# A two-layer hybrid block on one core: the state-space branch in groups of four time steps, every projection as three rounded products

## The chip, the cores and the metric

The kernel runs on one core of a Trainium2 chip. The core has a matrix engine (TensorE, PE in the profile, with its weight loads as PEld), a vector engine (DVE), a scalar engine (ACT), GpSimd (POOL) and a queue engine (SP) that issues most of the DMAs. Each engine works through its own queue in order and waits on semaphores for the others. The metric is the device time of one execution in microseconds (us); less is better.

## The reference

The input is 512 tokens of width 1024 with 16 learned tokens in front, all in 32-bit floating point. Two layers follow. Each layer normalizes, multiplies by `w_in` (1024 x 1376) and splits the result into three branches. Their results are normalized, joined, multiplied by `w_out` and added to the residual; then an MLP (1024 to 4096 and back, squared ReLU) follows. The branch that the change rewrites is the state-space one:

```
bu_re = einsum('blgc,gpc->blgp', uf, bb_re)      # 16 groups x 16 channels -> 64 states each
bu_im = einsum('blgc,gpc->blgp', uf, bb_im)
...
_, _, xr, xi = lax.associative_scan(_complex_affine_combine, (a_t_re, a_t_im, bu_re, bu_im), axis=1)
y = einsum('gcp,blgp->blgc', c_re, xr) - einsum('gcp,blgp->blgc', c_im, xi) + d_skip * uf
z = gelu(y);  out = z * sigmoid(z @ w_glu + b_glu)
```

So each complex state follows x[t] = lambda * x[t-1] + B u[t], one lambda for each of the 1024 states, and y[t] is the real part of C x[t], plus d u[t]. The other two branches are attention within a window of 128 and latent attention over all earlier tokens. Three of the gains in the inputs are some 3 to 8 times as large as usual, so that rounding shows in the output.

## The kernel before

Activations lie transposed: 128 features on the partitions, time along the free axis. The 528 rows of time (16 + 512) are two halves of 272 and 256, here called A and B (`hf` 0 and 1). Weights come from HBM in blocks of 128 output features. A block is two half-blocks, each a tile `raw` of 128 x 512 (256 KB) fetched by SP; there are 600 such loads.

`gemm` has two forms. In the **rounded** form a weight half-block is first split by `load_half`: ACT rounds it (`w` hi, line 123 by way of `act`), DVE subtracts to get the rest (`w` lo, line 132). The activation has been split likewise (`split`, `gains`). Three products per 128 features then run with rounded operands: hi*hi, hi*lo, lo*hi, so 12 matmuls per half-block (line 160). In the **exact** form, taken when the activation tile is plain F32, the 4 matmuls of a half-block run on unsplit 32-bit operands (line 152); no split is needed, and the profile shows each such matmul as two. Constants `FULL_IN`, `FULL_OUT` and `FULL_C0` say where the exact form stands: `w_in` of layer 0 for both halves (9 of 11 blocks for A, 11 for B), `w_out` for half A in both layers, and the first chunk of the MLP for half A in both layers. That makes 68 blocks or 136 half-blocks, 544 matmuls (1088 in the profile), 78 half-blocks of them before 295 us. After the first chunk `resplit` makes the split activation.

`s5_prep` builds, from 8 columns of parameters, a table `tab` of cos and sin for 272 time steps and the input matrices `b3`. `s5_half` then treats the 1024 states as 8 tiles of 128 and one time half at a time. For each tile: two matmuls make B u (line 472, from `u3`, a split copy of u made by ACT and line 466); DVE turns it by the table into real recurrences (lines 477 to 480), runs two scans along all time steps (line 485), turns back (488 to 491), and matmuls with C give y (line 497).

Order: `weave` emits a main stream of projection blocks and, between them, steps of two side streams, `s5_half` and `attn_half`, at rates `RS` and `RA`; the yields say what a step costs. The tile framework then orders instructions by priority and by free buffers; weight splits and norm chains carry a raised priority (`HW`, `HP`). The stages used below are: `w_in` A (0 to 54 us); `w_in` B woven with the branches of A (54 to 160); `w_out` A, first MLP chunk of A, woven with the branches of B (160 to 295); the rest of layer 0's MLP (295 to 590); then for layer 1 `w_in` A and a rest of layer 0 with the branches of A (590 to 750), `w_in` B, `w_out` A, MLP of A with the branches of B (750 to 970), and the MLP to the end.

Of the kernel before, what the change touches and what calls it, by code (L numbers as in the profile page):

```python
# [20 lines left out]
P = 128  # L21
# [24 lines left out]
TAB = 272  # L46
# [20 lines left out]
def hybrid(ctx, tc, xT, wblk, small, wglu, wuq, wukv, bD, cD, ident_d, bias_d, tbias_d, mask_d, rope_d, tau_d, outT):  # L67
# [26 lines left out]
    def f32(ap):  # L94
        return ap.bitcast(F32)
# [144 lines left out]
    def s5_prep(L):  # L240
# [17 lines left out]
        tau = tmp_p()[:, 0]  # L258
# [5 lines left out]
        for i in range(8):  # L264
            act(tab[:, 1, i, :], tau, scale=phi[:, i:i + 1])
        for i0 in range(0, 8, 2):
            x = tab[:, 1, i0:i0 + 2, :]
            km = tmp_q()
            V.tensor_scalar(km, x, MAGIC, None, op0=ALU.add)
            V.scalar_tensor_tensor(x, km, MAGIC, x, op0=ALU.subtract, op1=ALU.subtract)  # L270
            for i in range(i0, i0 + 2):
                V.scalar_tensor_tensor(tab[:, 1, i, :], tau, plo[:, i:i + 1], tab[:, 1, i, :], op0=ALU.mult, op1=ALU.subtract)
            V.tensor_scalar(km, x, MAGIC, None, op0=ALU.add)
            V.scalar_tensor_tensor(x, km, MAGIC, x, op0=ALU.subtract, op1=ALU.subtract)
# [4 lines left out]
        for i in range(0, 8, 4):  # L279
            x = tab[:, 0, i:i + 4, :]  # L280
            act(x, x, AF.Square)
            V.tensor_scalar(x, x, -2.0, 1.0, op0=ALU.mult, op1=ALU.add)
        ar, ai = sm(l, "are"), sm(l, "aim")
        nr, ni, den, cr, ci = t8("nr"), t8("nim"), t8("den"), t8("cr"), t8("ci")
        V.tensor_tensor(nr, r, tab[:, 0, :, 1], op=ALU.mult)
        V.tensor_scalar(nr, nr, 1.0, None, op0=ALU.subtract)
        V.tensor_tensor(ni, r, tab[:, 1, :, 1], op=ALU.mult)
# [5 lines left out]
        V.tensor_tensor(b, ni, ai, op=ALU.mult)  # L293
        V.tensor_tensor(cr, a, b, op=ALU.add)
        V.tensor_tensor(cr, cr, den, op=ALU.mult)
        V.tensor_tensor(a, ni, ar, op=ALU.mult)
# [3 lines left out]
        crb = cr.unsqueeze(2).to_broadcast([P, 8, 32])  # L300
        cib = ci.unsqueeze(2).to_broadcast([P, 8, 32])
        b3 = mk(mem, [96, 2, 8, P], F32R, "b3")
        braw = tmp_p().rearrange("p a t -> p (a t)")[:, :512].rearrange("p (c i j) -> p c i j", c=2, i=8)
        t12 = tmp_q().rearrange("p a t -> p (a t)")[:, :512].rearrange("p (c i j) -> p c i j", c=2, i=8)
        t1, t2 = t12[:, 0], t12[:, 1]
        nc.gpsimd.dma_start(out=braw, in_=bD[l])
        for c in range(2):
            hi = mk(wk, [P, 8, 32], F32R, "u3")
            V.tensor_tensor(t1, braw[:, c], crb, op=ALU.mult)
            V.tensor_tensor(t2, braw[:, 1 - c], cib, op=ALU.mult)  # L310
            V.tensor_tensor(t1, t1, t2, op=ALU.subtract if c == 0 else ALU.add)
            act(hi, t1)
            for q in range(2):
                iq = slice(4 * q, 4 * q + 4)
                bb = tmp_p().rearrange("p a t -> p (a t)")[:, :384].rearrange("p (i j c) -> p i j c", i=4, j=3)
                act(bb[:, :, 0, :], f32(hi[:, iq]))
                act(bb[:, :, 1, :], f32(hi[:, iq]))
                V.tensor_tensor(bb[:, :, 2, :], t1[:, iq], f32(hi[:, iq]), op=ALU.subtract)
                ps = mk(psm, [P, 512], F32, "pt")
                for j in range(4):  # L320
                    PE.transpose(ps[:96, j * P:(j + 1) * P], bb[:, j].rearrange("p a b -> p (a b)"), ident)
                act(b3[:, c, iq, :], ps[:96].rearrange("p (j m) -> p j m", j=4))
        ct = mk(mem, [P, 2, 8, 32], F32, "ct")
        nc.gpsimd.dma_start(out=ct, in_=cD[l])
        L["s5"] = dict(r=r, tab=tab, b3=b3, ct=ct)
# [40 lines left out]
    def w_in(L, hf, ar, M):  # L366
# [17 lines left out]
        for b in range(NB_IN):  # L384
# [3 lines left out]
            if b < 2:  # L388
                scaled(M["u"][:, b, :n], ps[:, :n])
# [650 lines left out]
```

## Time and profile before

| | us |
|---|---|
| median of 3 runs | 1323.53 (1322.12 to 1324.77) |
| profiled execution, first to last instruction | 1320.8 |
| PE busy | 1246.2 (94%) |
| DVE busy | 911.0 (69%) |
| ACT busy | 830.8 (63%) |
| mean DMA rate | 129 GB/s |

No time of the profiled execution other than its span is recorded; the median stands 2.7 us above it. A line of the grouped view ends in "busy, mean ns of one | idle before". The matmul lines count a 32-bit matmul twice. Matmuls overlap, so their mean length is longer than the distance from one to the next; the timeline gives the distance, as a run of so many in so many us.

### The profile page before, as it was taken

The page shows a single profiled execution, that of the slowest core. Times are in us where ns is not written, and L with a number is a line of the kernel's source. Part 1 is how long each engine was busy: PE and PEld are TensorE (multiplying, and loading weights), DVE is VectorE, ACT ScalarE, POOL GpSimd, SP SyncE. Part 2 cuts the span into 40 slices and gives each one's busy share as a digit, 9 for nine tenths or more (in the row PEclk, how much of TensorE's full clock was granted, in tenths as well). Part 3 has the DMA queues.
Part 4 walks back from the last instruction along what each step waited for, and adds up shares of the span by engine and source line. Part 5 has one row for each costly group of instructions (what it writes and reads, how often), then busy time and mean ns, then how long its engine had stood idle before and what let it go on. Part 6 is the DMA issues. An engine that isn't in the chain of part 4 may idle for free.

```text
span 1320.8 us, 24423 instructions
## 1 busy us (share of the span) xinstructions
PE 1246.2 (94%) x8760; PEld 1106.6 (84%) x8760; DVE 911.0 (69%) x2234; ACT 830.8 (63%) x1959; POOL 30.3 (2%) x64
## 2 busy tenths in 40 slices
PE   6999897999999999899999997999899999999985
PEld 5866664779999999898889987767789999999985
DVE  8699888757756656868998668796575333334776
ACT  5855758587765656856878656477676542534663
POOL 3001000000000000000000000000000000000000
PEclk9999999999999999899999998999899999999998
DMA  7422131345666666464344654312346433334653
GB/s 233 142 80 65 57 88 33 90 131 154 183 184 176 176 175 174 133 178 118 113 129 136 185 141 138 112 56 73 105 127 198 117 93 96 97 96 123 188 178 96
DMA packets 93240, 170.55 MB, mean 129 GB/s; under 512 B 10832, under 2 KB 14032, under 8 KB 93120
## 3 DMA queue, kind: packets, MB, share of 16 engines
q1 hardware_dynamic: 90288, 161.72, 43.0%
q0 software_dynamic: 2832, 7.28, 1.8%
q8 instruction: 69, 1.13, 0.4%
q14 instruction: 51, 0.42, 0.1%
HBM read 166.87 MB, written 2.10 MB: 128 GB/s over the span
## 4 chain that ended last, share of the span: by engine, by line
PE 73%; DVE 13%; ACT 10%; issue 2%; DMA 2%; DVEq 0%; ACTq 0%; POOLq 0%
PE d L160 45%; PE d L152 9%; PE bu L160 7%; PE o L703 2%; PE pt L679 2%; PE y L497 2%; ACT ch L123 2%; ACT slot L123 2%; DMA raw<-in_wblk 1%; PE s L623 1%; DVE big L730 1%; PE s L655 1%; DVE wQ L485 1%; DVE h L731 1%; ACT w L123 1%
## 5 line engine op out<-in xcount | busy, mean ns | idle before, releaser
L160 PE MATMUL d<-slot,w 128*128 128x256 f32 (+1 forms) x5568 | 704.5, 286 | 24.4 <-ACT ch L123 6.7
L160 PEld LDWEIGHTS d<-slot,w 128*128 128x128 f32 x5568 | 682.6, 190 | 39.6 <-ACT slot L123 8.4
L123 ACT ACTIVATE w<-raw 128x512 fp32r<-128x512 f32 x464 | 290.9, 628 | 255.4 <-PE d L160 182.5
L132 DVE TENSOR_TENSOR w<-raw,w 128x512 fp32r<-128x512 f32 x464 | 319.0, 690 | 183.5 <-ACT w L123 177.4
L152 PE MATMUL d<-slot,raw 128*128 128x256 f32 (+1 forms) x1088 | 272.0, 393 | 12.3 <-DMA raw<-in_wblk 10.5
L152 PEld LDWEIGHTS d<-slot,raw 128*128 128x128 f32 x1088 | 202.1, 192 | 55.7 <-ACT ch L123 10.5
L167 DVE TENSOR_TENSOR slot<-rl,slot 128x256 fp32r<-128x256 f32 (+1 forms) x112 | 47.1, 426 | 65.5 <-ACT slot L123 64.9
L160 PE MATMUL bu<-slot,w 128*128 128x256 f32 x768 | 92.2, 279 | 0.0
L160 PEld LDWEIGHTS bu<-slot,w 128*128 128x128 f32 x768 | 90.8, 188 | 0.0
L123 ACT ACTIVATE rl<-d 128x256 f32<-128x256 f32 (+1 forms) x112 | 42.1, 376 | 31.4 <-PE d L152 15.1
L197 DVE TENSOR_TENSOR ch<-ch 128x256 f32<-128x256 f32 (+1 forms) x112 | 47.4, 424 | 14.2 <-ACT ch L123 12.6
L123 ACT ACTIVATE slot<-rl 128x256 fp32r<-128x256 f32 (+3 forms) x128 | 52.7, 420 | 2.8
L123 ACT ACTIVATE slot<-h,small 128x256 fp32r<-128x256 f32 (+3 forms) x88 | 39.6, 503 | 14.3 <-DVE h L731 10.3
L123 ACT ACTIVATE ph<-pt 128x512 f32<-128x512 f32 (+2 forms) x66 | 36.4, 552 | 18.9 <-PE pt L679 13.8
L123 ACT ACTIVATE rl<-rl 128x256 f32<-128x256 f32 (+1 forms) x112 | 45.9, 418 | 2.1
L801 DVE TENSOR_TENSOR big<-d,big 128x256 f32<-128x256 f32 (+1 forms) x80 | 34.2, 428 | 15.0 <-PE d L160 11.8
L123 ACT ACTIVATE big<-d 128x256 f32<-128x256 f32 (+1 forms) x64 | 23.8, 373 | 19.7 <-PE d L152 13.3
L655 PE MATMUL s<-kv,slot 96*128 96x264 f32 (+3 forms) x80 | 27.0, 419 | 5.8 <-DVE mx L534 5.8
L123 ACT ACTIVATE ch<-big 128x256 f32<-128x256 f32 (+1 forms) x64 | 26.2, 412 | 9.4 <-DVE big L801 7.2
L623 PE MATMUL s<-kv,slot 128*128 128x512 f32 (+1 forms) x64 | 31.3, 570 | 0.8 <-DVE mx L534 0.5
L123 ACT ACTIVATE u<-slot 32x272 fp32r<-32x272 f32 (+1 forms) x64 | 26.9, 420 | 4.9 <-PE bu L472 2.3
L731 DVE SCALAR_TENSOR_TENSOR h<-big,small,h 128x256 f32<-128x256 f32 (+1 forms) x64 | 28.4, 481 | 0.0
(583 smaller groups left out, 1242.3 us busy)
## 6 DMA issues: line engine op xcount, KB each, us to landing
raw<-in_wblk SPq DMA_DIRECT2D x600, 256.0 KB, 2.7
ph<-in_wuq POOLq DMA_DIRECT2D x8, 256.0 KB, 3.1
h<-in_xT SPq DMA_DIRECT2D x4, 272.0 KB, 4.0
h<-in_xT SPq DMA_DIRECT2D x1, 1024.0 KB, 12.4
ph<-in_wukv POOLq DMA_DIRECT2D x4, 256.0 KB, 3.4
u<-in_wglu POOLq DMA_DIRECT2D x4, 256.0 KB, 3.1
out<-h SPq DMA_DIRECT2D x1, 1024.0 KB, 5.6
out<-h SPq DMA_DIRECT2D x4, 256.0 KB, 2.1
```

Of the source, the lines that this page charges most:

```text
L123: S.activation(out, in_, func, **kw)
L132: V.tensor_tensor(w[:, 1].rearrange("p k m -> p (k m)"), raw, f32(hi), op=ALU.subtract)
L152: PE.matmul(ps[:, :n], lhsT=raw[:, k * P:(k + 1) * P], rhs=a[:, 4 * q + k, :n], start=q + k == 0, stop=q + k == 4)
L160: PE.matmul(ps[:, :n], lhsT=w[:, wi, k, :], rhs=a[:, ai, 4 * q + k, :n], start=i == 0, stop=i == 23)
L167: V.tensor_tensor(lo, src, f32(hi), op=ALU.subtract)
L197: V.tensor_tensor(acc, acc, sq, op=ALU.add)
L497: PE.matmul(yps[j:j + 32, :n], lhsT=s5["ct"][:, c, i - 1 + e, :], rhs=xs[e][:, c, :n], start=c == 0, stop=c == 1, tile_position=(0, j))
L623: PE.matmul(sp[:, :2 * nk].rearrange("p (e k) -> p e k", e=2), lhsT=M["q"][:, c0:c0 + P], rhs=L["k2"][:, :, ks:ks + nk], start=True, stop= ...
L655: PE.matmul(sp, lhsT=M["qh"][0:96, 2 * g + e, o:o + P], rhs=L["kh"][:, 2 * g + e, c0:c1], start=True, stop=True)
L679: PE.transpose(pt[:, 256 * x + P * e:256 * x + P * e + P], vs[e][:, c0:c0 + P], ident)
L731: V.scalar_tensor_tensor(h[hf][:, k, o:o + n], src[:, k, :n], sm(l, gn, k), h[hf][:, k, o:o + n], op0=ALU.mult, op1=ALU.add)
L801: V.tensor_tensor(ac[:, b, :n], ps[:, :n], ac[:, b, :n], op=ALU.add)
```

## The change

Two things change together. First, the three `FULL_` constants become empty, so that every block of `gemm` takes the rounded form: 600 half-blocks are split by ACT and DVE, before it was 464. Second, `s5_prep` and `s5_half` work on groups of four time steps (`CL`): u is laid out by step within the group, a matmul with slices of the identity stacks the four steps on the partitions, the scan runs over 68 or 64 groups, four tiles side by side in one instruction (its multiplier is zero at each tile's start), and y within a group comes from a matrix `tt` for the inputs of the group and four matrices `vt` for the state before it. The table shrinks from 272 to 72 columns; `s5_prep` multiplies out lambda's powers on DVE (`cmul`). These matmuls are plain 32-bit ones. The rates `RS` change too.

```diff
-FULL_IN = ((0, 0), (0, 1))
-FULL_OUT = ((0, 0), (1, 0))
-FULL_C0 = ((0, 0), (1, 0))
-RS = ((5.4, 3.56), (1.8, 4.4))
+FULL_IN = ()
+FULL_OUT = ()
+FULL_C0 = ()
+RS = ((2.4, 1.5), (0.75, 2.2))
...
-TAB = 272
+CL = 4
+TAB = 72
...
+        def cmul(dst, src, fr, fi, iq):
+            ni = iq.stop - iq.start
+            pq = flat(tmp_q(), 128 * ni)
+            p4, q4 = (pq[:, 64 * ni * e:64 * ni * e + 64 * ni].rearrange("p (c i j) -> p c i j", c=2, i=ni) for e in range(2))
...
+            for c in range(2):
+                V.tensor_tensor(p4[:, c], src[c], frb, op=ALU.mult)
+                V.tensor_tensor(q4[:, c], src[c], fib, op=ALU.mult)
+            V.tensor_tensor(dst[0], p4[:, 0], q4[:, 1], op=ALU.subtract)
+            V.tensor_tensor(dst[1], p4[:, 1], q4[:, 0], op=ALU.add)
...
+        for i0 in range(0, 8, 4):
+            iq = slice(i0, i0 + 4)
+            ws = [flat(tmp_p(), 512).rearrange("p (i s j) -> p i s j", i=4, s=CL) for _ in range(2)]
+            at = lambda m: [w[:, :, CL - 1 - m, :] for w in ws]
+            cmul(at(0), [braw[:, c, iq] for c in range(2)], cr, ci, iq)
+            for m in range(1, CL):
+                cmul(at(m), at(m - 1), lr, li, slice(i0, i0 + 4))
             for c in range(2):
                 ps = mk(psm, [P, 512], F32, "pt")
                 for j in range(4):
...
+                    PE.transpose(ps[:, j * P:(j + 1) * P], ws[c][:, j].rearrange("p a b -> p (a b)"), ident)
+                act(wt[:, c, iq, :], ps.rearrange("p (j m) -> p j m", j=4))
...
+        for m in range(CL):
+            for i0 in range(0, 8, 4):
+                iq = slice(i0, i0 + 4)
+                cmul([vt[:, m, c, iq] for c in range(2)], [vt[:, (m - 1) % CL, c, iq] for c in range(2)], lr, li, iq)
...
+        for o in range(2):
+            ups = mk(psm, [P, 512], F32, "y")
+            for j in range(4):
+                for q in range(CL):
+                    PE.matmul(ups[32 * q:32 * q + 32, j * K:j * K + K], lhsT=ident[:, 32 * j:32 * j + 32],
+                              rhs=M["u"][:, o, q * K:q * K + K], start=True, stop=True, tile_position=(0, 32 * q))
+            act(u4[:, o, :n], ups[:, :n])
...
             for c in range(2):
-                iv = 0.0 if hf == 0 else it[:, c, i:i + 1]
-                V.tensor_tensor_scan(v_[:, c, :n], rb, w_[:, c, :n], iv, op0=ALU.mult, op1=ALU.add)
...
+                V.tensor_tensor_scan(v_[:, c, :n], rs[:, 4 * o * K:4 * o * K + n], w_[:, c, :n], 0.0, op0=ALU.mult, op1=ALU.add)
...
+            for q in range(CL):
+                for m in range(3):
+                    for j in range(4):
+                        i = 4 * o + j
+                        if m == 0:
+                            lt, rh = s5["tt"][:, i, q, :], u4[:, o, j * K:j * K + K]
+                        else:
+                            lt, rh = s5["vt"][:, q, m - 1, i, :], x_[:, m - 1, j * K:j * K + K]
+                        PE.matmul(yps[32 * j:32 * j + 32, q * K:q * K + K], lhsT=lt, rhs=rh, start=m == 0, stop=m == 2,
+                                  tile_position=(0, 32 * j))
```

The scheduler's order changes with it. On PE, at the end of `w_in` A of layer 0 (`d_347` is its last block, `d_613` and `d_709` the first of B, `pt` the transposes of `s5_prep`), there stood before:

```order
L160 MATMUL d_347<-slot_293,w_350 128x272 x12
L160 MATMUL d_347<-slot_293,w_367 128x272 x12
L202 MATMUL d_601<-ch_584,ones 128x256
L202 MATMUL o_665<-am_663,ones 128x272
L152 MATMUL d_613<-slot_575,raw_614 128x256 x4
L152 MATMUL d_613<-slot_575,raw_620 128x256 x2
L321 MATMUL pt_523<-ident,wP_519 96x128 x4
L152 MATMUL d_613<-slot_575,raw_620 128x256 x2
L321 MATMUL pt_533<-ident,wP_529 96x128 x4
L152 MATMUL d_709<-slot_575,raw_710 128x256 x2
```

In the changed kernel, at the same place (`pt` the transposes of `s5_prep`, `y_707` the product that gives `tt`; the fence begins behind the first three sets of these), there stand:

```order
L341 MATMUL pt_794<-ident,wP_759 128x128 x4
L494 MATMUL y_966<-slot_159,ident 32x68
L203 MATMUL d_914<-ch_897,ones 128x256
L161 MATMUL d_926<-slot_880,w_929 128x256 x12
L161 MATMUL d_926<-slot_880,w_946 128x256 x12
L494 MATMUL y_966<-slot_159,ident 32x68 x15
L161 MATMUL d_1066<-slot_880,w_1069 128x256 x5
L494 MATMUL y_984<-slot_159,ident 32x68 x16
```

All 20 rows of the transposes and of `tt` now stand between the last block of A and the norm sum `d_914` that the first block of B needs; before, blocks of B stood between the transposes.

On DVE, in the same place of the program, before (`slot` u and the branch inputs, `wP`, `wQ` the state-space temporaries; no weight split stands here):

```order
L371 TENSOR_TENSOR slot_610<-d_613,rc_600 128x256
L562 SCALAR_TENSOR_TENSOR slot_151<-slot_151,small_92,am_663 128x272
L466 TENSOR_TENSOR u_95_628<-slot_151,u_95_628 32x272 x2
L477 TENSOR_TENSOR wP_639<-bu_636,tab_444 128x544
L478 TENSOR_TENSOR wQ_640<-bu_636,tab_444 128x544
L479 TENSOR_TENSOR wP_639<-wP_639,wQ_640 128x272
```

And in the changed kernel (`vt` the output matrices of `s5_prep`, `ch` the norm sum of half B, `w_929` the first weight split of B):

```order
L316 TENSOR_TENSOR wQ_822<-vt_697,lam_679 128x128
L198 TENSOR_TENSOR ch_897<-ch_897 128x256
L133 TENSOR_TENSOR w_929<-raw_927,w_929 128x512
L198 TENSOR_TENSOR ch_897<-ch_897 128x256
L317 TENSOR_TENSOR vt_697<-wQ_822 128x128
L198 TENSOR_TENSOR ch_897<-ch_897 128x256
L318 TENSOR_TENSOR vt_697<-wQ_822 128x128
L198 TENSOR_TENSOR ch_897<-ch_897 128x256
```

The norm sum and the first split of B now stand among the 96 small products of `s5_prep`, 58 of which lie ahead of the norm sum's first row.

## Rows read from the trace of the kernel before

**Rows 1.** The page: the span, then busy time, share and count of PE

```profile
span 1320.8 us, 24423 instructions
PE 1246.2 (94%) x8760; PEld 1106.6 (84%) x8760; DVE 911.0 (69%) x2234; ACT 830.8 (63%) x1959; POOL 30.3 (2%) x64
```

**Rows 2.** The page: the chain that ended last, shares by line

```profile
PE d L160 45%; PE d L152 9%; PE bu L160 7%; PE o L703 2%; PE pt L679 2%; PE y L497 2%; ACT ch L123 2%; ACT slot L123 2%; DMA raw<-in_wblk 1%; PE s L623 1%; DVE big L730 1%; PE s L655 1%; DVE wQ L485 1%; DVE h L731 1%; ACT w L123 1%
```

**Rows 3.** Busy time by stretch: PE, PEld, DVE, ACT, POOL, then PE's granted clock

```profile
0.00:54.00 54.00, 42.02 (x195) 35.27 (x196) 39.01 (x134) 35.19 (x68) 13.66 (x31) 1.00 0.69 212
54.00:160.00 106.00, 97.85 (x523) 67.05 (x524) 93.25 (x307) 68.92 (x207) 6.08 (x12) 0.98 0.22 65
160.00:295.00 135.00, 126.12 (x630) 89.53 (x628) 101.93 (x312) 97.64 (x246) 5.24 (x11) 0.96 0.30 86
295.00:590.00 295.00, 287.14 (x2228) 280.78 (x2228) 199.83 (x384) 195.99 (x415) 1.05 (x2) 0.99 0.61 170
590.00:750.00 160.00, 158.63 (x1217) 140.66 (x1216) 136.92 (x349) 118.30 (x303) 2.17 (x4) 1.00 0.46 134
750.00:970.00 220.00, 206.11 (x1249) 169.63 (x1248) 152.17 (x386) 136.90 (x336) 2.13 (x4) 0.96 0.38 109
970.00:1321.00 351.00, 328.36 (x2729) 323.64 (x2727) 187.88 (x365) 177.87 (x389) 0.00 (x0) 0.98 0.45 128
```

**Rows 4.** Groups by line: weight splits on ACT and DVE, u's copy on ACT

```profile
L123 ACT ACTIVATE w<-raw 128x512 fp32r<-128x512 f32 x464 | 290.9, 628 | 255.4 <-PE d L160 182.5 <-PE bu L160 43.5 <-ACT ch L123 11.8
...
L123 ACT ACTIVATE u<-slot 32x272 fp32r<-32x272 f32 x32 | 13.7, 427 | 2.3 <-issue 1.6 <-PE bu L472 0.2
...
L132 DVE TENSOR_TENSOR w<-raw,w 128x512 fp32r<-128x512 f32 x464 | 319.0, 690 | 183.5 <-ACT w L123 177.4
```

**Rows 5.** Timeline of PE: start, length, instructions (the matmul's pace)

```profile
22.01 25.93 PE L152 MATMUL d<-slot,raw 128*128 128x272 f32 x112 [1.47 <-DVE slot L371]
47.58 6.36 PE L160 MATMUL d<-slot,w 128*128 128x272 f32 x48
...
780.20 10.52 PE L152 MATMUL d<-slot,raw 128*128 128x256 f32 x48
```

**Rows 6.** The chain in order of time: pace at 256 columns, table functions of layer 1

```profile
1168.39 5.60 PE d L160 x48
...
285.94 2.02 ACT tab L123
...
293.07 2.02 ACT tab L276
```

**Rows 7.** Groups by line: the state-space work of DVE, and a 128-wide product

```profile
L485 DVE TENSOR_TENSOR_SCAN wQ<-pr,wP 128x272 f32<-128x272 f32 x32 | 22.2, 711 | 0.0
...
L477 DVE TENSOR_TENSOR wP<-bu,tab 128x544 f32<-128x544 f32 x16 | 11.4, 715 | 0.6 <-PE bu L472 0.5
...
L480 DVE TENSOR_TENSOR wP<-wP,wQ 128x272 f32<-128x272 f32 x16 | 6.9, 433 | 0.0
...
L466 DVE TENSOR_TENSOR u<-slot,u 32x272 fp32r<-32x272 f32 x16 | 6.9, 431 | 1.8 <-ACT u L123 1.5
...
L318 DVE TENSOR_TENSOR wP<-wQ,u 128x128 f32<-128x128 f32 x8 | 2.2, 283 | 0.0
```

**Rows 8.** Timeline: small 32-bit matmuls on parts of the array, and two 128-wide DVE products

```profile
95.11 0.66 PE L703 MATMUL o<-ph,vs 128*64 128x128 f32 x8 [0.25 <-ACT ph L123]
...
96.45 0.14 PEld L497 LDWEIGHTS y<-wP,ct 128*32 128x32 f32 x4 [0.39 <-DVE nm L537]
...
96.45 0.65 PE L497 MATMUL y<-wP,ct 128*32 128x272 f32 x4
...
59.70 0.48 DVE L318 TENSOR_TENSOR wP<-wQ,u 128x128 f32<-128x128 f32 x2
```

**Rows 9.** Timeline of PE: behind an idle stretch

```profile
227.82 1.70 PE L655 MATMUL s<-kv,slot 96*128 96x400 f32 x2 [4.62 <-DVE mx L534]
...
234.02 5.03 PE L152 MATMUL d<-slot,raw 128*128 128x272 f32 x16
```

More of the change, by code (lines that the diff above doesn't have):

```diff
@@ L257, in s5_prep @@
         tab = mk(mem, [P, 2, 8, TAB], F32, "tab")
-        tau = tmp_p()[:, 0]
+        tau = tmp_p()[:, 0, :TAB]
         if l == 0:
@@ L307, in s5_prep, with flat @@
[L307 to L318, printed above, removed]
+        def flat(t, n):
+            return t.rearrange("p a t -> p (a t)")[:, :n]
@@ L319, in s5_prep @@
+        t3 = mk(psm, [P, 512], F32, "y")
+        for i0 in range(0, 8, 4):
[5 more added lines that the diff above has]
+                cmul(at(m), at(m - 1), lr, li, slice(i0, i0 + 4))
+            for c in range(2):
                 ps = mk(psm, [P, 512], F32, "pt")
@@ new lines, in s5_prep @@
+            for j in range(4):
+                i = i0 + j
+                for c, rhs in enumerate((vt[:, CL - 1, 0, i, :], nci[:, i, :])):
+                    PE.matmul(t3[:, 32 * i:32 * i + 32], lhsT=ws[c][:, j].rearrange("p a b -> p (a b)"), rhs=rhs,
+                              start=c == 0, stop=c == 1)
+        t3v = t3[:, :256].rearrange("p (i j) -> p i j", i=8)
+        act(tt[:, :, 3, :], t3v)
+        for so in range(3):
+            for q in range(so + 1):
+                f = 32 * (q + 3 - so)
+                act(tt[32 * q:32 * q + 32, :, so, :], t3v[f:f + 32])
@@ L327, in norm_in @@
+        for m in range(CL):
+            for i0 in range(0, 8, 4):
+                iq = slice(i0, i0 + 4)
+                cmul([vt[:, m, c, iq] for c in range(2)], [vt[:, (m - 1) % CL, c, iq] for c in range(2)], lr, li, iq)
+        L["s5"] = dict(r4=r4, rs=rs, tab=tab, wt=wt, vt=vt, tt=tt)
     def norm_in(l, hf, n, tag):
@@ L524, in s5_half @@
         act(e_, e_, AF.Exp, scale=-1.0)
-        V.tensor_tensor(yv, z, e_, op=ALU.mult)
+        for o in range(2):
+            V.tensor_tensor(y[:, o, :n].rearrange("p (k q) -> p q k", q=CL), z[:, o].rearrange("p (q k) -> p q k", q=CL),
+                            e_[:, o].rearrange("p (q k) -> p q k", q=CL), op=ALU.mult)
         yield 2.0
@@ L966, in _consts @@
     rope = np.stack([np.tile(np.concatenate([c, c]), (4, 1)), np.tile(np.concatenate([-s, s]), (4, 1))], 1).astype(np.float32)
-    tau = np.tile(np.arange(TAB, dtype=np.float32)[None], (P, 1))
+    steps = np.concatenate([np.arange(1, CL), CL * np.arange(TAB - CL + 1)])
+    tau = np.tile(steps.astype(np.float32)[None], (P, 1))
     return ident, bias, tb, mask, rope, tau
```

161 lines of the change are left out of this document (81 added, 80 removed).

## The prediction

> **What bounds the kernel now.** I first read the page: PE is busy 94% of a span of 1320.8 us, DVE 69%, ACT 63% [rows 1]. The chain of waits agrees, with 45% of the span on rounded matmuls (line 160, tile `d`), 9% on exact ones (line 152) [rows 2]. But these are means over stages of different kinds, so the second view is the busy time by stretch [rows 3]. From 295 to 590 us and from 970 on, PE and its weight loads (PEld) are busy 92 to 97% and DVE near 60%: PE alone sets the time. In the woven stages that is not so. From 54 to 160 us PEld is busy 67 of 106 us and DVE 93 (88%); from 160 to 295 PEld 89.5 of 135, DVE 102 and ACT 98; from 590 to 750 PE 159, PEld 141 and DVE 137 of 160. There PE waits in small pieces for softmax, norms and the state-space branch, and work saved on PE alone buys little. From 750 to 970 PE has 206 of 220 and DVE 152, so PE leads again.
>
> **Exact blocks to rounded ones.** A weight split costs ACT 0.628 us and DVE 0.690 us [rows 4]. On PE an exact matmul of 272 columns takes twice 25.93/112 = 0.463 us and three rounded ones 3 x 6.36/48 = 0.398 [rows 5], so 0.066 us is saved; at 256 columns it is 2 x 10.52/48 = 0.438 [rows 5] against 3 x 5.60/48 = 0.350 [rows 6], so 0.088. By stage that is 72 x 0.066 = 4.8 us in 0 to 54, 88 x 0.088 = 7.7 in 54 to 160, 152 x 0.066 = 10 in 160 to 295, 40 x 0.066 = 2.6 in 295 to 590, 192 x 0.088 = 16.9 in 750 to 970: 42 us of PE in all. Against it stand 136 more splits, 94 us of DVE and 85 of ACT.
>
> **State-space branch.** On DVE one tile of 128 states costs four products of 0.715, four of 0.433, two scans of 0.711 and the rest of u, 0.431 [rows 7]: 6.45 us, for 8 tiles 52 us per half. After, the same chain without the last term runs twice per half on 544 columns: 12 us and some 1.6 of small ones. So DVE is relieved of 38 us per half, 152 in all. ACT loses 16 copies of 0.427 per half [rows 4], 6.8 us. `s5_prep` gains 96 products of 128 columns a layer, 96 x 0.283 = 27 us of DVE [rows 7], or 96 x 0.2 = 19 if they run as closely as the two in 0.48 us [rows 8]. Strided accesses over four time steps have no row; between the 0.433 of the same columns and the 0.715 of twice as many I take the lower, which is the same element count (4 per half, 1 us at stake).
>
> On PE the branch had per half 16 matmuls of line 472 (0.12 us each by the pace above) and 32 profile rows of line 497, four of which take 0.65 us with their tail [rows 8]: about 5.5 us. After there are 144 matmuls or 288 profile rows of 68 columns; alone each takes 0.463/2 x 68/272 = 0.058 us. 256 of them stand on a quarter of the array each. Rows of half and quarter width do overlap in pairs: 8 of 128 columns end in 0.66 us, where one after the other they need 8 x 0.109 = 0.87 and a tail [rows 8]. Four together give 256 x 0.058/4 + 32 x 0.058 = 5.6 us, no overlap gives 16.7, hence 0 to 44 us over four halves. I take 0, nearest to the overlap shown. Changes between 32-wide and full-width pieces number 60 after and 72 before, by the order on PE. The Trainium skill, TensorEngine Tiling, Key Properties, says that a change of tiling mode drains the engine; the four rows' 0.65 us against 4 x 0.116 alone leaves 0.2 at most for it [rows 8], so 12 us and 14 us, no difference that counts.
>
> **The sum by stages,** against 1320.8 us.
> - 0 to 54: 4.8 us saved, one split (0.63 + 0.69) later at the start: -3.4.
> - 54 to 160: DVE 93 - 38 + 22 x 0.69 + 8 rests of the activation x 0.433 + some 24 of `s5_prep` = 98 us; ACT 69 + 22 x 0.628 - 6.8 = 76 [rows 3, 4, 7]. DVE stays the fullest, and its own share of before, 88%, gives 111 us, 95% gives 103. In its queue 58 of the small products now stand ahead of the norm sum that the first block of B waits for, with no other work for PE in that place: 58 x 0.2 = 12 us and the norm chain, 15 to 20 us of idle PE. Since DVE works through it, it is contained in the 98. What is added is the clock: behind a wait of 4.6 us 16 matmuls took 5.03 us, 0.314 each against 0.2315 [rows 9, 5], so +1.3 us. I take 0 for the stage, bounds -5 and +15.
> - 160 to 295: DVE 102 - 38 + 38 x 0.69 + 24 x 0.433 = 101; ACT 98 + 38 x 0.628 + 16 x 0.427 - 6.8 = 122 us of 135, now the fullest at 90%. The saving of 10 us on PE meets that: 0, bounds -7 and +26.
> - 295 to 590: -2.6; and two table functions of layer 1 on the chain, 2.02 us each for 2176 columns [rows 6], have 576: about -2.5. Together -5.
> - 590 to 750: DVE 137 - 38 + 27 = 126. PE stays bound by its own work. 64 of layer 1's small products stand in one block without a split between, 13 us, with 44 rounded matmuls (5 us) of PE work ahead: 8 us of wait, against what DVE's relief gives back of the 19 us in which no weights load: 0.
> - 750 to 970: 16.9 us off PE. DVE 152 - 38 + 48 x 0.69 + 24 x 0.433 = 157, ACT 137 + 48 x 0.628 = 167 of 220, neither full. But each block now waits for a split queued behind softmax and scans: I count 12 of the 17.
> - 970 on: nothing.
>
> Sum -3.4 + 0 + 0 - 5 + 0 - 12 = -20, so 1300.4. The median of the runs stands 2.7 above the span, hence **1303 us**.
>
> **Rivals.** *The splits choke layer 0's woven stages (slower).* The exact form spared DVE and ACT where they were fullest. If the relief of the state-space branch falls where PE or ACT is late anyway, the 60 splits there cost DVE their 60 x 0.69 = 41 us: 1320.8 + 41 - 20 + 2.7 = 1344. It decides once idle PE between 54 and 295 us grows by over 20 us. For it: DVE and ACT at 88 and 72% there, ACT going to 90%, and splits that queue in order behind scans and softmax. Against: from 590 to 750 us rounded blocks ran between the same branches with DVE at 86% and PE at 99% [rows 3].
>
> *The serial state-space chain was what held the woven stages (much faster).* Then they shrink to their fullest engine at some 95%: 98 to 101 us (-5), 122 to 128 (-7), 590 to 750 -10 of the 19 without loads, and 750 to 970 the whole 17 and 8 of idle PE. With -3.4 and -5 that is -55: 1268. For it: 8 chains of two scans become two. Against: the softmax chains remain.
>
> *The small matmuls do not overlap.* Then up to 44 us of PE come in, of which the stages led by DVE hide about a quarter: 1303 + 33 = 1336. The Trainium skill, TensorE: Matmul & The Clock Gate, Part 3, says a weight load overlaps running matmuls only where the row groups differ; all these tiles use all rows. The trace speaks against it: four loads of line 497 end in 0.14 us ahead of matmuls of 0.65 us [rows 8], but only two tiles took part.
>
> That the change does not do what it says I exclude: no row of the exact line stands in the new order of PE.
>
> **Chances.** Forecast 0.55 (its own range 1288 to 1324), choked by splits 0.20, much faster 0.15, no overlap 0.10. No change is within 0.2%, 1321 to 1326, about what a measurement of this kernel can tell. Faster: 0.15 and 0.51 of the forecast, 0.66; same 0.05; slower 0.29. The range 1272 to 1340 leaves out a bit of each end.
>
> **What will show it.** Right: no exact rows; 600 splits on ACT and DVE; DVE's scan line with 16 rows instead of 64; 750 to 970 shorter by some 12 us; a gap of 15 to 20 us on PE near 50 us, then matmuls at the lower clock for a few us. Total DVE nearly unchanged (-152 + 94 + 54 and the rests), ACT near 880. Wrong: PE waiting for `w` for more than 20 us within the woven stages; small matmuls further apart than 0.03 us; or a woven stage shorter than its fullest engine's sum here.

## The result and the profile after

The changed kernel took 1353.32 us in the median of 4 runs (1351.2 to 1355.68), the kernel before 1322.82 in 4 runs beside it: a ratio of 1.0229 (95% interval 1.0214 to 1.0245). The forecast was 1303 with a range from 1272 to 1340, so it was wrong in sign and in range. The page of the changed kernel, span and busy time:

```profile
span 1350.6 us, 27902 instructions
PE 1235.6 (91%) x10328; PEld 1154.1 (85%) x10328; DVE 902.8 (67%) x2318; ACT 869.0 (64%) x2030; POOL 32.3 (2%) x66
```

Against [rows 1] PE is busy 10.6 us less, DVE 8 less, ACT 38 more. DVE and ACT came out about as forecast; on PE 42 us less work was forecast. Yet the span grew by 30 us: PE waits more, and works more slowly. Up to its last matmul, PE (weight loads included) is idle 101.0 us instead of 60.8. The stretches in which its granted clock was 0.50, the lower of its two levels (1.2 GHz), sum to 119.2 us of the span instead of 53.6 (10 and 13 of them at the very end, where no matmul runs). PE's busy time within them is 66.7 us instead of 30.0; if that counts half, PE's work at the full clock fell from 1231.2 to 1202.3 us, by 29 (an estimate).

To see where, the ends of the same piece of work are compared. A "half-block" is counted by the matmuls of its tile; the table gives what the changed kernel lost in each stage of the prediction, by the end of the half-block that closes the stage in the kernel before. Three of the experiments below stand beside it.

| stage (time before) | forecast | changed | products alone | branch alone | no subtraction |
|---|---|---|---|---|---|
| 0 to 54 | -3.4 | -2.0 | -1.5 | +0.1 | -5.8 |
| 54 to 160 | 0 | +8.5 | +37.9 | +3.5 | +2.7 |
| 160 to 295 | 0 | +9.8 | +12.0 | +3.1 | +10.2 |
| 295 to 590 | -5 | +1.9 | +5.0 | -2.7 | -5.0 |
| 590 to 750 | 0 | +3.7 | +0.4 | +3.3 | +3.7 |
| 750 to 970 | -12 | +3.2 | +10.5 | -5.4 | -7.2 |
| 970 to the last block | 0 | +4.6 | +1.6 | +3.7 | +0.5 |

How much side work stands ahead of a given half-block differs from run to run, so that some us move between neighbouring stages: within 750 to 970 the changed kernel is 35.0 us late at half-block 414 and 25.1 at the stage's end. The sums over all stages do not depend on that.

The same three stretches of work by their windows (from half-block 18 to 78, to 114, and 348 to 450; columns as in [rows 3]), in the kernel before:

```profile
48.00:288.00 240.00, 222.97 (x1170) 156.98 (x1169) 201.01 (x635) 163.65 (x454) 12.38 (x25) 0.97 0.27 79
288.00:349.00 61.00, 58.70 (x380) 52.83 (x379) 43.39 (x107) 48.66 (x103) 0.00 (x0) 1.00 0.57 163
752.00:997.00 245.00, 228.08 (x1386) 188.94 (x1385) 175.20 (x441) 156.77 (x385) 2.13 (x4) 0.97 0.39 113
```

and in the changed kernel:

```profile
46.00:300.00 254.00, 216.81 (x1906) 178.26 (x1905) 192.25 (x680) 186.65 (x499) 12.45 (x24) 0.91 0.25 74
300.00:367.00 67.00, 59.74 (x451) 58.39 (x450) 52.04 (x134) 49.76 (x105) 0.90 (x3) 0.92 0.51 145
775.00:1025.00 250.00, 221.80 (x1816) 196.56 (x1815) 175.13 (x438) 175.64 (x421) 2.15 (x4) 0.93 0.39 111
```

In all three PE's share and its mean clock fell, and no engine is full: DVE has 76, 78 and 70%, and in the first and third it is busy no longer than before (192 and 175 us against 201 and 175). DVE's sum alone does not make these stretches longer.

The first large gap is the one that the forecast counted at nothing, the preparation of layer 0. Timeline of the changed kernel (in brackets the idle time of the engine and what ended it):

```profile
55.21 1.28 PE L203 MATMUL o<-am,ones 128*128 128x272 f32 x2 [3.31 <-ACT am L124]
...
59.32 1.12 PE L341 MATMUL pt<-ident,wP 128*128 128x128 f32 x4 [2.84 <-DVE wP L317]
...
63.30 0.29 DVE L318 TENSOR_TENSOR wP<-wQ 128x128 f32<-128x128 f32 x1 [2.63 <-PE y L346]
...
71.75 1.03 ACT L124 ACTIVATE ch<-h 128x256 f32<-128x256 f32 x3 [2.65 <-PE y L346]
...
77.63 0.44 PE L494 MATMUL y<-slot,ident 128*32 128x68 f32 x2 [5.00 <-ACT tt L124]
```

PE and DVE take turns here. The second set of products cannot start until PE has read the first (63.30); the norm of half B cannot start until PE has read the negated C, because both use the buffer `ch` (71.75); the first matmul for u waits for the copies of `tt` (77.63). From 51.9 to 78.6 us no block of weights runs; PE is idle between its small matmuls, and from 53.8 us its granted clock is 0.50. The window for it, of the kernel before and then of the changed one:

```profile
60.00:80.00 20.00, 19.44 (x88) 13.32 (x88) 18.07 (x41) 11.34 (x29) 0.56 (x1) 1.00 0.30 92
```

```profile
60.00:80.00 20.00, 12.21 (x56) 11.08 (x55) 13.93 (x58) 8.20 (x21) 0.00 (x0) 0.50 0.05 14
```

Half-block 24 ends at 83.0 us instead of 59.3. Of these 23.7 us 17 are won back by half-block 46 (6.5 late), and 10 are lost again by half-block 82 (16.3 late). The other kind of gap stands at norm chains, as twice in layer 1:

```profile
800.40 1.22 PE L161 MATMUL d<-slot,w 128*128 128x256 f32 x4 [4.83 <-DVE w L133]
...
821.76 0.76 DVE L781 TENSOR_TENSOR big<-big,ch 128x256 f32<-128x256 f32 x2
...
827.60 3.26 DVE L171 SCALAR_TENSOR_TENSOR slot<-h,small,slot 128x256 fp32r<-128x256 f32 x8
...
832.80 2.90 PE L161 MATMUL d<-slot,w 128*128 128x256 f32 x12 [10.47 <-DVE slot L422]
```

At 800 us PE waits for a weight split, at 833 for DVE to read out a finished block; both stand in DVE's queue behind or among the residual and norm of a half (16 operations of lines 781 and 782, and 8 of line 171, the rest of the split activation; 9.1 us without a pause from 821.76). The first gap is new: half-block 363, which waits there, was exact before. The second is older: half-block 375 was rounded before too, and PE waited 6.67 us for it:

```profile
803.80 2.47 PE L160 MATMUL d<-slot,w 128*128 128x256 f32 x10 [6.67 <-ACT ch L123]
```

Both rows of the changed kernel lie at a granted clock of 0.50: the second has 8 matmuls more and is 1.68 us longer, 0.21 us each, against 5.60/48 = 0.117 [rows 6].

### The profile page after: what moved, and what is told of

It is laid out like the page before. It is cut to its first block, busy times and chain, and to the rows that moved or that the text cites. A ratio compares the mean times of both kernels' runs of the same rounds, so it can differ in the third digit from the quotient of the medians.

```text
span 1350.6 us, 27902 instructions
## 1 busy us (share of the span) xinstructions
PE 1235.6 (91%) x10328; PEld 1154.1 (85%) x10328; DVE 902.8 (67%) x2318; ACT 869.0 (64%) x2030; POOL 32.3 (2%) x66
## 4 chain that ended last, share of the span: by engine, by line
PE 75%; DVE 13%; ACT 9%; issue 2%; DMA 1%; DVEq 0%; ACTq 0%; POOLq 0%
PE d L161 56%; PE bu L161 7%; PE o L754 2%; PE s L674 2%; PE pt L730 2%; ACT ch L124 2%; DVE slot L171 2%; DVE big L781 2%; DVE h L782 2%; DVE w L133 2%; ACT slot L124 1%; PE s L640 1%; ACT w L124 1%; PE o L203 1%; PE bu L508 1%
## 5 line engine op out<-in xcount | busy, mean ns | idle before, releaser
L161 PE MATMUL d<-slot,w 128*128 128x256 f32 (+1 forms) x7200 | 955.7, 291 | 55.3 <-DVE slot L422 13.5
L161 PEld LDWEIGHTS d<-slot,w 128*128 128x128 f32 x7200 | 909.1, 193 | 79.4 <-DVE w L133 13.9
L124 ACT ACTIVATE w<-raw 128x512 fp32r<-128x512 f32 x600 | 376.7, 629 | 301.5 <-PE d L161 231.9
L133 DVE TENSOR_TENSOR w<-raw,w 128x512 fp32r<-128x512 f32 x600 | 413.9, 691 | 232.0 <-ACT w L124 225.3
L168 DVE TENSOR_TENSOR slot<-rl,slot 128x256 fp32r<-128x256 f32 (+1 forms) x128 | 54.2, 429 | 69.0 <-ACT slot L124 67.9
L124 ACT ACTIVATE slot<-rl 128x256 fp32r<-128x256 f32 (+1 forms) x128 | 52.9, 420 | 2.6
L852 DVE TENSOR_TENSOR big<-d,big 128x256 f32<-128x256 f32 (+1 forms) x80 | 34.3, 428 | 14.3 <-PE d L161 10.5
L124 ACT ACTIVATE slot<-h,small 128x256 fp32r<-128x256 f32 (+1 forms) x72 | 33.0, 506 | 12.6 <-DVE h L782 8.4
L124 ACT ACTIVATE ch<-h 128x256 f32<-128x256 f32 (+1 forms) x64 | 25.0, 414 | 15.8 <-DVE ch L198 9.5
L171 DVE SCALAR_TENSOR_TENSOR slot<-h,small,slot 128x256 fp32r<-128x256 f32 (+1 forms) x72 | 31.7, 492 | 0.0
L754 PE MATMUL o<-ph,vs 128*64 128x128 f32 x256 | 25.2, 287 | 0.7 <-ACT big L124 0.7
```

Source lines behind the costliest of these rows:

```text
L124: S.activation(out, in_, func, **kw)
L133: V.tensor_tensor(w[:, 1].rearrange("p k m -> p (k m)"), raw, f32(hi), op=ALU.subtract)
L161: PE.matmul(ps[:, :n], lhsT=w[:, wi, k, :], rhs=a[:, ai, 4 * q + k, :n], start=i == 0, stop=i == 23)
L168: V.tensor_tensor(lo, src, f32(hi), op=ALU.subtract)
L171: V.scalar_tensor_tensor(lo, src, gain, f32(hi), op0=ALU.mult, op1=ALU.subtract)
L754: PE.matmul(ops[64 * e:64 * e + 64, :P], lhsT=v, rhs=pp[:, P * e:P * e + P], start=i == 0, stop=i == len(ph) - 1, tile_position=(0, 64 * e))
```

## The experiments

Medians of 4 to 10 runs; the ratio is to runs of the kernel before made beside them.

| run | median us | ratio (95% interval) |
|---|---|---|
| e1 products only | 1387.41 | 1.0489 (1.0473 to 1.0504) |
| e2 branch only | 1327.84 | 1.0039 (1.0025 to 1.0053) |
| e3 preparation woven | 1348.80 | 1.0203 (1.0188 to 1.0218) |
| e4 own buffer | 1354.95 | 1.0243 (1.0228 to 1.0258) |
| e5 no rest | 1323.51 | 1.0008 (0.9999 to 1.0017) |
| e6 rest on GpSimd | 1396.77 | 1.0557 (1.0540 to 1.0575) |
| e7 branch woven, exact blocks | 1321.40 | 0.9995 (0.9986 to 1.0005) |
| e8 first chunk exact | 1342.36 | 1.0154 (1.0139 to 1.0169) |
| e9 as e7, weights shifted | 1317.90 | 0.9964 (0.9951 to 0.9977) |
| e10 before, weights shifted | 1326.71 | 1.0028 (1.0018 to 1.0038) |
| e11 splits first | 1348.68 | 1.0190 (1.0169 to 1.0211) |
| e12 `w_in` exact | 1348.44 | 1.0194 (1.0180 to 1.0208) |

**e1 and e2, each part alone.** Theory A: the preparation costs the 30 us. Theory B: the splits do. e1 keeps the old rates `RS`, e2 has the new ones.

```diff
-FULL_IN = ((0, 0), (0, 1))     # e1, in the kernel before
-FULL_OUT = ((0, 0), (1, 0))
-FULL_C0 = ((0, 0), (1, 0))
+FULL_IN = ()
+FULL_OUT = ()
+FULL_C0 = ()
...
-FULL_IN = ()     # e2, in the changed kernel
-FULL_OUT = ()
-FULL_C0 = ()
+FULL_IN = ((0, 0), (0, 1))
+FULL_OUT = ((0, 0), (1, 0))
+FULL_C0 = ((0, 0), (1, 0))
```

> The kernel before with the three FULL_ tables empty, so that all 600 weight half-blocks are split, and the old state-space branch. Theory A (the 30 us come from the new preparation of layer 0, which holds the matrix engine from 51.9 to 78.6 us): without that preparation the rounded form costs little, 1315 to 1330 us. Theory B (the 136 more splits choke ACT and DVE in the woven stages): 1340 to 1355 us, with over 20 us more idle time on PE between 54 and 295 us than the 18 us of before there. If A and B share it, 1330 to 1340.

> The changed kernel with the three FULL_ tables of before (68 exact blocks), new state-space branch, new rates. Theory A: the layer-0 preparation still stands ahead of the blocks of B on PE, so about +20 us at that place, some of it won back later: 1330 to 1345 us. Theory B: with the splits gone only the relief of DVE is left, 1295 to 1312 us.

The products alone cost 64 us, the branch alone 4.7. Beside the new branch the products cost 25 us, so the new branch with its rates is worth 34 us to a kernel that splits everything, and nothing to one with exact blocks. Both runs missed every stated range: e1 is 32 us above that of B, e2 lies 2 us below that of A. A falls as the main cause; B is larger than expected. The rates were never changed by themselves, so what they contribute is not known. What it looks like in e1, at the end of `w_in` A, by a window and by two rows of the timeline:

```profile
44.00:52.00 8.00, 8.00 (x67) 8.00 (x66) 8.00 (x21) 3.25 (x5) 1.06 (x2) 1.00 0.75 201
```

```profile
55.67 2.02 ACT L123 ACTIVATE tab<-tab 128x2176 f32<-128x2176 f32 x1 [5.80 <-DVE tab L274]
...
70.66 1.19 PE L202 MATMUL d<-ch,ones 128*128 128x256 f32 x2 [18.26 <-DVE pa L292]
```

The rounded `w_in` A keeps DVE full (8.00 of 8 us), and the table of the old branch, which before was made beside exact blocks, comes late; half B's activation stands behind it on ACT, and PE idles 18 us.

**e3 and e4, the preparation.** e3 spreads it between the blocks of B, e4 gives the negated C a buffer of its own.

```diff
-        nci = chain_tmp()[0][:, :256].rearrange("p (i j) -> p i j", i=8)
+        nci = (chain_tmp()[0] if l else mk(nt, [P, 272], F32, "rl", bufs=2))[:, :256].rearrange("p (i j) -> p i j", i=8)
...
 # e3 alone, cut: s5_prep yields after each set of products (2.0), tt (0.5), each power of vt (0.8)
+RS0 = (3.2, 0.75)
-        weave(s1(), ((s5_half(L, M[0]), RS[l][0], 0), (attn_half(L, M[0]), RA[l][0], 0)))
+        weave(s1(), ((seq(prep, s5_half(L, M[0])), RS0[l], 0), (attn_half(L, M[0]), RA[l][0], 0)))
```

> The changed kernel with the heavy part of the preparation of layer 0 (the 96 products, transposes, tt) emitted as the first steps of the state-space side stream between the blocks of B, at rate 3.2 instead of 2.4, and the negated C in a buffer of its own. Theory A: PE no longer idles 27 us at 52 to 79 us; of it 12 us had been won back by 200 us anyway, so 1330 to 1341 us in all, and half-block 24 ends at about 63 us (59.3 before, 83.0 after the change). Theory B: the time stays within 5 us of 1353, the wait only moves.

> The changed kernel, with the negated C of layer 0's preparation in a buffer that the norm of B does not use (one name changed; the order on PE of the preparation stays). Theory A1 (the norm of B, which evicts the first blocks of B, waited until the preparation's last product because both use the buffer ch): the wait of 5.0 us on PE at 72.6 us goes and the norm is done before 70 us: 5 to 8 us less, 1345 to 1349. Theory A2 (the place of the preparation in PE's queue alone holds it): 1350 to 1355, no change.

In e3 half-block 24 ends at 56.1 us, so the gap is gone there, but half-block 30 is already 15.8 us behind the kernel before, and only 4.5 us of the time are gained: the wait moved. e4 changed nothing measurable in the time, and A1 falls. Its trace shows why:

```profile
55.31 1.01 ACT L124 ACTIVATE ch<-h 128x256 f32<-128x256 f32 x3
...
68.87 0.42 DVE L198 TENSOR_TENSOR ch<-ch 128x256 f32<-128x256 f32 x1
```

ACT's part of the norm of B starts 16 us earlier than in the changed kernel, but DVE's part still stands behind the small products in DVE's queue, and the norm sum behind the transposes in PE's. The first block of B starts at 77.0 us instead of 78.7. So the order of the two queues, and not the buffer alone, held the blocks.

**e5 and e6, the subtraction alone.** For the 136 half-blocks that were exact before (`old`), the rest `w` lo is not computed (e5; their third product takes the rounded weights in its place), or computed on GpSimd (e6).

```diff
             act(hi, raw)
-            V.tensor_tensor(w[:, 1].rearrange("p k m -> p (k m)"), raw, f32(hi), op=ALU.subtract)
+            if not old:                                        # e5
+                V.tensor_tensor(w[:, 1].rearrange("p k m -> p (k m)"), raw, f32(hi), op=ALU.subtract)
...
-                        PE.matmul(ps[:, :n], lhsT=w[:, wi, k, :], rhs=a[:, ai, 4 * q + k, :n], start=i == 0, stop=i == 23)
+                        PE.matmul(ps[:, :n], lhsT=w[:, 0 if old else wi, k, :], rhs=a[:, ai, 4 * q + k, :n], start=i == 0, stop=i == 23)
...
+            (nc.gpsimd if old else V).tensor_tensor(w[:, 1].rearrange("p k m -> p (k m)"), raw, f32(hi), op=ALU.subtract)   # e6
```

> The changed kernel without DVE's subtraction in the 136 half-blocks that were exact before: their third product takes the rounded weights again in place of the rest, so 136 x 0.691 = 94 us of DVE are left out, while ACT's copy, all matmuls and all waits on ACT stay. Theory D (DVE's time for the splits is what chokes): most of the 25 us that the products cost beside the new state-space branch come back, 1325 to 1333 us. Theory E (the blocks wait for ACT and for norm chains as such, now that no block runs without a split): 1345 to 1354 us. Between: both.

> The changed kernel with the subtraction of those same 136 half-blocks on GpSimd, which is busy 32 of 1351 us. No row shows what 128x512 takes there. Theory D: if it takes under 2 us, nearly the time of the run without the subtraction, 1325 to 1340. Theory E, or a subtraction there of over 3 us: 1350 or more, since each half-block of 1.4 us of PE would wait for it.

e5 gives back 30 us, all of what the change cost, with every rounded matmul and every copy of ACT still there. Its windows for the same three stretches:

```profile
42.00:291.00 249.00, 218.94 (x1904) 180.01 (x1904) 160.08 (x608) 184.74 (x495) 12.77 (x26) 0.90 0.26 76
291.00:351.00 60.00, 56.45 (x446) 55.41 (x444) 43.14 (x120) 47.80 (x100) 0.53 (x2) 0.97 0.55 162
758.00:994.00 236.00, 213.91 (x1819) 190.67 (x1818) 146.07 (x392) 173.52 (x420) 2.14 (x4) 0.96 0.40 118
```

The last stretch falls from 250 to 236 us, the middle one from 67 to 60, the first by 5. So ACT's part of a split was hidden, although ACT was the fullest engine of the forecast's third stage; DVE's part was not, although DVE was at 70 to 78%. The range of D is met (e5 is 1.5 us faster still), and E falls in the form that it has here. What the 30 us consist of is read from e5's page and from the view of waits (us in total, times, longest), for the kernel before, the changed one and e5:

```profile
PE 1223.3 (93%) x10328; PEld 1143.2 (87%) x10328; DVE 823.7 (62%) x2182; ACT 867.0 (66%) x2032; POOL 32.1 (2%) x66
```

```profile
PE d L160 <- DVE w L132: 3.5, 2, 2.4
```

```profile
PE d L161 <- DVE w L133: 12.1, 7, 4.8
```

```profile
PE d L162 <- DVE w L134: 4.2, 4, 2.3
```

With the same 10328 rows, PE is busy 12 us less in e5 than in the changed kernel (1223.3 against 1235.6), and idle 18 us less (82.9 against 101.0). Of the 12 some 11 are the clock: 45.2 us of PE's work stand at the lower clock instead of 66.7, and half of the difference is counted (an estimate). Of the 18 only 8 are waits that end with a subtraction (12.1 less 4.2); the rest are waits for other things. But e5 takes away two things at once, DVE's time and the wait of the third product for DVE, and does not separate them. Nor does it close every gap: the one behind half-block 374, 10.47 us in the changed kernel, stands in e5 too. In e2 and e8 the 8 operations of line 171 are missing from the chain, since the chunk after it is exact, and the gap there is 6.7 and 6.9 us. So the split of the activation has a price of its own, which e5 leaves in:

```profile
810.29 2.05 PE L162 MATMUL d<-slot,w 128*128 128x256 f32 x8 [10.33 <-DVE slot L423]
```

e6 was to separate the two, since it keeps the wait and frees DVE. It came out 43 us slower than the changed kernel and missed what D gave for a subtraction of under 2 us (1325 to 1340). Groups by line of e6, GpSimd and DVE, then of the changed kernel, then two rows of e6's timeline:

```profile
L133 POOL TENSOR_TENSOR w<-raw,w 128x512 fp32r<-128x512 f32 x136 | 183.7, 1358 | 367.9 <-ACT w L124 360.6 <-PE pt L730 5.5 <-DMA raw<-in_wblk 0.2
...
L198 DVE TENSOR_TENSOR ch<-ch 128x256 f32<-128x256 f32 x77 | 38.8, 503 | 15.7 <-ACT ch L124 14.0
```

```profile
L198 DVE TENSOR_TENSOR ch<-ch 128x256 f32<-128x256 f32 x77 | 32.6, 424 | 8.1 <-ACT ch L124 6.8
```

```profile
182.61 1.26 POOL L133 TENSOR_TENSOR w<-raw,w 128x512 fp32r<-128x512 f32 x1 [2.52 <-ACT w L124]
...
182.79 1.11 DVE L588 TENSOR_SCALAR nm<-mx 128x2 f32<-128x2 f32 x1
```

One subtraction takes 1.36 us there, twice DVE's, and DVE's 2182 instructions take 909.6 us in e6 and 823.7 in e5, so nearly all that was taken off DVE came back. The mean of 503 ns hides two cases. The 67 of these 77 that no GpSimd subtraction overlaps take 421 ns as always; the 10 that one overlaps take 1.06 us on average, as if held until the subtraction is done. The second row, on 2 columns, takes 1.11 us where its group takes 0.165 in the changed kernel. The Trainium skill, GPSIMD Engine Reference, section 1, says that GpSimd's SBUF interfaces are shared with VectorE, and that it contends with VectorE instructions in a two-port mode or with two SBUF inputs. The trace agrees for those with two inputs; in which mode the one-input row ran no run shows. That DVE's time comes back would explain a return to the changed kernel's 1353 us; the 43 us on top were not followed up.

**e8, e11, e12: which blocks, and in what order.** e8 puts back the exact form in the first MLP chunk of A, e12 in layer 0's `w_in`; e11 raises the splits' priority over that of the norm chains.

```diff
-FULL_C0 = ()                       # e8
+FULL_C0 = ((0, 0), (1, 0))
-FULL_IN = ()                       # e12
+FULL_IN = ((0, 0), (0, 1))
-HW = 50                            # e11
+HW = 150
```

> The changed kernel with the exact form back in the first MLP chunk of A alone (64 half-blocks, FULL_C0 as before). By the ends of the half-blocks, the rounded form cost 8 us more between half-blocks 78 and 108 and some 8 between 426 and 450 than the exact form beside the same branch. Theory E (exact blocks are cover for the norm chains around them): those 16 us come back, 1335 to 1343 us. Theory D (the DVE time of 64 splits, 44 us, spread over two stages in which DVE is busy 70%): 1345 to 1352.

> The changed kernel with the exact form back in w_in of layer 0 alone (40 half-blocks, FULL_IN as before). The two tables FULL_IN and FULL_OUT together should be worth 14 us, what the first MLP chunk left of the 25. Theory D: the 40 splits come off DVE in the stretch up to 160 us where DVE is busy 88 to 96% and the preparation waits for it: 1339 to 1347 us. Rival (the loss up to 160 us is the preparation's own and is won back by 300 us in any case): 1350 to 1354.

> The changed kernel with the priority of the weight splits raised from 50 to 150, above that of the norm chains (100). Theory D1 (a split comes late because it stands behind a norm chain in DVE's and ACT's queues; there is time enough for both): fewer gaps on PE, 1335 to 1348 us. Theory D2 (the time itself is missing: what the splits gain, the chains lose): 1350 to 1360.

e8 gains 11 us, e12 4.9; what is left of the 25 to `FULL_OUT` is 10, if they add up (it was not run alone). e8 lies at the upper end of what theory E gave, and below D, which spread 44 us of DVE over two stages. The E of this run, exact blocks as cover for the norm chains around them, is not the one that e5 refuted, since the half-blocks of e5 wait for DVE no more than exact ones do. e12 lies between both its ranges, and decides nothing. e11 gains 4.6 us, 0.7 short of what D1 gave and 1.3 below D2: the order of splits and norm chains explains a part, and what the rest of the loss is due to it does not show.

**e7, e9, e10: a better version, and a surprise.** e7 is e2 with the preparation of both layers woven as in e3. e9 and e10 move the weight buffers.

```diff
+    pad = ctx.enter_context(tc.tile_pool(name="pad", bufs=1))    # ahead of wraw and wsp
+    V.memset(pad.tile([P, 96], F32, tag="pad", name="pad"), 0.0)  # e9, in e7: 384 bytes
+    V.memset(pad.tile([P, 32], F32, tag="pad", name="pad"), 0.0)  # e10, in the kernel before: 128 bytes
```

> The new state-space branch with the exact blocks of before, and the preparation of both layers woven between blocks (rates 3.2 and 0.95). The new branch with exact blocks took 1327.8. The blocks in layer 0 that are exact can run beside the preparation without DVE, so the 16 us lost by half-block 24 and the 7.5 us lost at half-block 276 should not arise. Theory A for what is left of the branch: 1316 to 1324 us. Rival (the branch of A comes later and the end of the stage with it, as when the preparation was woven among rounded blocks): 1325 to 1330.

> The version with the exact blocks, the new branch and the woven preparation (1321.4 us), with a pad of 384 bytes a partition ahead of the weight buffers, so that raw and w lie at the addresses that they had before the change (w at 183168 instead of 182784). In all runs with the new branch the 256-column rounded matmuls followed each other at 117.9 to 118.4 ns, in those with the old branch at 116.7 to 117.2; some 4,600 of them here. Theory F (it is the place of the weight buffers): the pace goes back to 116.7 to 117.2 and the time to 1315 to 1318. Rival (something else of the new branch, as the program's size or the place of another tile): pace 118 and 1320 to 1323.

> The kernel before with a pad of 128 bytes a partition ahead of the weight buffers (w at 183296, a multiple of 512, as 182784 is; before at 183168). Theory F: the pace of the 256-column rounded matmuls goes from 117.0 to some 118 ns and the time up by 4 to 6 us, 1326 to 1329. Rival: no change, 1321 to 1324.

e7 met theory A: it is 6.4 us faster than e2, and no faster than the kernel before (ratio 0.9995). From half-block 18 to 78 it reads:

```profile
48.00:287.00 239.00, 224.88 (x1683) 168.78 (x1682) 145.77 (x560) 150.06 (x414) 13.29 (x26) 0.97 0.26 79
```

DVE works 146 us where it worked 201 before, and the stretch is as long as before, 239 us: beside exact blocks DVE's sum did not set this time. The buffers' addresses follow from the program: the tiles of the new branch take 384 bytes less of a partition than the old ones, which moved `raw`, `w` and all that lies behind them. The activation's slots, which feed the matmuls, stayed. The chain in order of time, in the two-activation MLP, gives 48 matmuls of 256 columns in the changed kernel, e9 and e10 (before: 5.60 [rows 6]):

```profile
1124.05 5.68 PE bu L161 x48
```

```profile
1124.51 5.60 PE bu L164 x48
```

```profile
1122.29 5.68 PE bu L162 x48
```

Theory F's forecasts hold both ways: e9 is the fastest version, 0.36% below the kernel before, and e10 makes the kernel before 3.4 us slower with only the pad added. From half-block 450 to 536, the two-activation MLP, the changed kernel, e2, e5, e7 and e10 all take 2.8 us more than the kernel before, e1 and e9 0.1 and 0.0. But one pace in each kernel, as the expectation of e9 has it, is not what the traces show: half-blocks at about 0.1167 and at about 0.1184 us stand side by side in all of them, and a move turns some the other way. Half-blocks 110 to 125 take 22.88 us in the kernel before and 22.56 in e10; half-blocks 128 to 140 take 18.36 and 18.62. Of the half-blocks whose matmuls follow each other evenly, 203 run at the faster pace and 61 at the slower before, 47 and 223 in e10, 58 and 246 in the changed kernel, 211 and 67 in e9.

## Why the prediction was wrong

- *The sums for DVE and ACT* were right: DVE 902.8 (forecast nearly unchanged from 911), ACT 869 (near 880), no exact rows, 16 scans, 600 splits. *PE's sum* was not: of the 42 us 29 came (the estimate above), mainly since the new branch, taken at 0, adds 9 us of PE (e2 against before, 1254.8 and 1246.2, with nearly the same time at the lower clock).
- *The small matmuls* overlap, as taken. In the chain of the changed kernel 32 matmul rows on a quarter of the array took 0.61 us, 19 ns each, while 16 rows on the whole array took 1.93:

```profile
84.34 0.61 PE y L494 x32
84.96 1.93 PE bu L508 x16
```

  That rival (1336) falls. The sum for one half is higher than the 5.6 us forecast, since the 32 whole-array rows take 0.12 us each and not 0.058: some 3.9 us for them and 4.9 for the 256 small ones. (The 0.116 us that the prediction gives for a row of line 497 "alone" is half of the 0.2315 of [rows 5]. Four rows alone would take 0.93 us, more than the 0.65 shown, so [rows 8] give no figure for a change of tiling. Nothing hangs on that, as both kernels change about equally often.)
- *"Since DVE works through it, it is contained in the 98"* (54 to 160 us) failed. DVE did not work through it: PE and DVE waited for each other, 27 us without a block, where 15 to 20 were expected. The clock cost more than the 1.3 us written down. The 16 matmuls of rows 9 that gave this price are only the last piece of a low stretch: in the kernel before the granted clock is 0.50 from 226.2 to 236.4 us, and they start at 234.02. In the changed kernel it stayed at 0.50 from 53.8 to 81.1 us. Yet this error is small in the end: without the preparation's gap 4.5 us come back (e3), or 6.4 beside exact blocks (e7).
- *"I take 0"* for 54 to 160 and *0* for 160 to 295: the two cost 8.5 and 9.8 us, within the bounds given. In e5 12.9 of the 18.3 remain, in e2 6.6, so the weight subtractions are a part of this loss and the preparation another. The rest stays open.
- *"I count 12 of the 17"* (750 to 970) and -5 (295 to 590) are the steps that failed by most: +3.2 and +1.9, 15 and 7 us off. The forecast compared DVE's sum with the stage, 157 of 220 us, put the waits for splits at 5 of the 17 us in the one stage, and at nothing in the other. e5 shows that DVE's subtractions were what took the gain: without them these two stages give -7.2 and -5.0, near the forecast. The largest single piece lies at half-blocks 363 to 366, where the changed kernel loses 9.3 us against e5: the wait of 4.83 us at 800 us and the low clock behind it. The reading that fits is that the exact blocks had been work for PE that needed nothing from DVE while DVE was busy with a chain of 6 us or more; e7 and e8 speak for it, but no run shows it by itself.
- *The rival "the splits choke"* named the operation, and was given 0.20 and 1344. One of its signs came, idle PE grown by 20 us (17 to 37 us of the first stretch above); the other, over 20 us of waits for `w` in the woven stages, did not: the waits that the whole trace puts down to DVE's `w` are 12.1 us. It had the price from DVE's time (41 us for 60 splits) but only in layer 0; by e5 the subtractions cost 5 us in the woven stretch of layer 0, 4 ahead of it, 7 in the first chunk behind it and 14 in layer 1.
- *"The serial state-space chain was the limit"* falls: with exact blocks and the new branch the time is that of before (e7).
- *Not foreseen at all*: the branch's tiles moved the weight buffers, worth 3.4 us by e10. Of the +4.6 from 970 us on 2.8 are this pace, in the two-activation MLP; 2.1 lie ahead of half-block 450, where e5 gains 1.9 instead.

So of the 30 us, 25 are the products beside the new branch (1353.3 less e2's 1327.8), and 4.7 the branch with its rates: 3.4 for the place of the buffers and 6.4 for the preparation, less some 5 won elsewhere, if these add up. That DVE's subtractions in the formerly exact half-blocks make up the loss is shown by e5. Whether by the time that they take from DVE's other work or by the wait of the matmuls for them, and how much each single chain contributes, was not separated.

## What to carry to other kernels

A slower form of a matmul that needs nothing from the other engines can be worth more than a faster one that does: before replacing it, ask what PE runs while DVE is in its longest uninterrupted chain. Judge an added operation by what stands behind that chain and what PE needs next, not by DVE's share of a stage; take the operation out in an experiment, and its price shows at once. And lay a new one-off preparation between blocks instead of ahead of them (4.5 us in e3, 6.4 in e7).

## What the hardware showed unexpectedly

- The place of the weight buffers in SBUF changes the pace of 256-column rounded matmuls: in the two-activation MLP, with the first tile `w` at 182784 or 183296 bytes 48 take 5.68 us, at 183168 they take 5.60, with the same instructions. It is not a better place as such: other half-blocks run faster at 183296 (110 to 125, above), and at 182784 half-blocks 110 to 125 run at the slower pace in the changed kernel and at the faster one in e7. What decides between the two paces is open. At 272 columns the pace is 0.125 us in all of these runs. Only these three places were tried.
- A subtraction on GpSimd holds up DVE operations that fall into it, to 1.06 us instead of 0.42, and even one of 2 columns to 1.11 us.
- PE's idle time is paid twice: the same matmuls follow each other at 0.21 us instead of 0.118 until the clock is back, and the time at the lower clock more than doubled, from 53.6 to 119.2 us. In e5 some 11 of the 30 us regained are this second payment (the estimate above).
